# Second norm of a decoder block: the rounded and low parts of its transposed input made from SBUF, two tiles at a time

## The chip, the cores and the metric

One core of a Trainium2 chip runs the whole kernel. The core has TensorE (PE, matrix products into PSUM), VectorE (DVE), ScalarE (ACT), GpSimd (POOL) and SyncE (SP, which issues most transfers). Each engine works through its own list of instructions in order and waits on semaphores for the others. The metric is the device time of one execution in microseconds (us), the median of several runs. A profile of one execution gives every instruction's start and duration.

## What is computed

A decoder block on 512 positions of width 1024, in float32. What matters here is its second half: the attention and gMLP branches have been merged, and

```python
x = x + gate1 * (merged @ w_out)
h2 = rms_norm(x, norm2_g) * (1.0 + scale2) + shift2
f_g, f_u = jnp.split(h2 @ w_ffn_in, 2, axis=-1)      # w_ffn_in: 1024 x 5632
x = x + gate2 * ((jax.nn.silu(f_g) * f_u) @ w_ffn_out)
```

and a final RMSNorm. `scale2`, `shift2` and the gates come from the conditioning vector.

## The kernel before

**Products in three parts.** Every float32 product is made of three matmuls on fp32r numbers. An operand `a` is kept as a rounded part (`hi`, an fp32r copy of `a`) and a low part (`lo = a - hi`). `mm3` (L51 to L55) then adds `hi*hi`, one product of `hi` and `lo` (L54) and another (L55). So every tensor that TensorE reads has to be written twice, the rounded part mostly by ScalarE (an activation with function Copy), the low part mostly by VectorE (a subtraction).

**Weights.** The weights come in chunks of 128x1024 numbers through a stream with three raw buffers (L58 to L145). `ensure(i)` issues what has room and prepares all chunks up to `i`: ScalarE's rounded part at L110, the low part at L114, or, where a chunk's low part is marked "later", as a function kept in `do` that runs L112 when it is called. `W_F` are the four chunks of the first 256 columns of both halves of `w_ffn_in`; `WF0` lists them in order. All the other columns of `w_ffn_in` go through `s_issue(q)` (L1171) and `s_prep(q)` (L1194), for q = -2 to 17: each step takes two raw tiles, `ra` and `rb`, and makes sums and differences of their blocks (a Strassen-like scheme of seven block products), with ScalarE's rounded parts at L1206, L1215, L1223 and L1230 and VectorE's work at L1209 to L1211, L1218, L1219, L1226 and L1233. A raw buffer is free for the next transfer when its last reader is done.

**The output projection** (L1239 to L1272) runs over two halves of the positions (256 each) and, in each, over eight chunks of `w_out`, n_ = 0 to 7. In the second half the chunks come in the order of L1238: four for the first 512 columns, then four for the others. At the end of a column half `resid` (L1101) scales the product by the gate (L1104), adds it to the residual stream (L1105) and sums squares on ScalarE (L1106). `row_rstd` (L1108) makes the row's factor on VectorE (L1109) and GpSimd (L1110), and `norm2_x` (L1121) scales the rows into `xn`, one block of 128 rows on VectorE (L1128), the other on ScalarE (L1126). Between the chunks of the second half stand pieces of other work, written out by hand: the first half's norm and transposes, the preparation of `WF0`, and the start of `s_prep(-2)`.

**The transposes and what follows them** are `norm2_T` (L1130). For each of four banks k2 = 0 to 3 of PSUM (`x2T`, banks 4 to 7) TensorE makes four 128x128 transposes: two tiles kt = 2*k2 and 2*k2 + 1 of 128 columns, 256 positions each. From each tile three things are made:

- the rounded part `hi`, by ScalarE out of PSUM with scale and bias (L1159),
- `h2f`, the same in float32, by VectorE (L1164) or ScalarE (L1162), out of PSUM again,
- the low part `lo = h2f - hi`, by VectorE (L1165).

Instructions of two engines that read the same bank are ordered one behind the other by the kernel's tile framework. The banks of the first half are called in three pieces, at n_ = 2 of the second half's output projection, with the preparation of the chunk `WF0[2]` and `s_issue(-2)` between them. The second half's four banks are called as one, after the first chunk of the second weight half (L1477), and `pre[3]` (L1230, L1233) follows them.

**After it.** The first FFN columns are multiplied (`pf`, L1465 to L1491). `t_diff` (L1320) and `t_split` (L1328) then make the differences of `h2f` for the block products and split them into the tiles `tb`. Then comes the loop over q (L1500) with 20 steps of seven block products (`sprod`, 12 matmuls each), whose partial sums R are copied by ScalarE at L1533 to L1551 between the products that need them.

The order on every engine is that in which the instructions are written (a manual schedule), so moving a call moves its instructions on each engine's list.

Of the kernel before, what the change touches and what calls it, by code (L numbers as in the profile page):

```python
# [12 lines left out]
AF = mybir.ActivationFunctionType  # L13
OP = mybir.AluOpType
# [14 lines left out]
def block_kernel(ctx: ExitStack, tc: tile.TileContext, x, positions, w_ada, b_ada, w_in,  # L29
# [3 lines left out]
    T, V, A, P, SY = nc.tensor, nc.vector, nc.scalar, nc.gpsimd, nc.sync  # L33
# [8 lines left out]
    def bank(k, name="bank"):  # L42
        return psum.tile([128, 512], F32, name=name, tag=f"b{k}", bufs=1)

    def f(ap):
        return ap.bitcast(F32)
# [11 lines left out]
    stream, wseq, chunk = [], [], {}  # L58
# [58 lines left out]
    def ensure(upto):  # L117
        upto = min(upto, len(stream) - 1, st["limit"] - 1)
        while True:
            for i in range(st["prep"], min(st["prep"] + 16, len(stream), st["limit"])):  # L120
                if "raw" in stream[i]:
                    continue
                if room(i):
                    issue(i)
                elif stream[i]["kind"] == "w" or not stream[i]["mid"]:
                    break
            if st["prep"] > upto:
                break
            prep(st["prep"])
            st["prep"] += 1  # L130

    def room(i):
        e = stream[i]
        pend = stream[st["prep"]:i]
        if e["kind"] == "m" and e["early"]:
            return sum(p["kind"] == "m" for p in pend) < 8
        if e["kind"] == "m" and e["mid"]:
            return all(p["kind"] == "w" for p in pend) and len(pend) <= 1
        return sum(p["kind"] == "w" or not (p["early"] or p["mid"]) for p in pend) < RAWB


    def get(i, ahead=2):
        k = wseq.index(i)
        ensure(wseq[min(k + ahead, len(wseq) - 1)])
        return chunk[i]  # L145
# [128 lines left out]
    for i in range(4):  # L274
        t = base.tile([128, D], F32, name=f"x{i}", tag=f"X{i}", bufs=1)
# [202 lines left out]
    for kt in range(8):  # L478
        hi, lo = chunk[W1[kt]]
# [210 lines left out]
    def opt_a_mm(o, tk, hi, lo, kts, lhs, K, first=True):  # L690
        for j, kt in enumerate(kts):
            a = tuple(t[:, tk * 128:(tk + 1) * 128] for t in lhs[kt])
            mm3(o, a, (hi[:, j], lo[:, j]), kt == 0 and first, kt == K - 1, skip_group_check=True)
# [113 lines left out]
    for g in range(4):  # L807
        pb = [bank2(b, "pav") for b in nbanks()]
        for i in W_AV[g]:
# [10 lines left out]
            hi, lo = get(i)  # L820
# [280 lines left out]
    def resid(p, c0, n, slot, tk, gate):  # L1101
        cs_ = slice(c0, c0 + n)
        t = t512("rt")
        V.tensor_mul(t[:, :n], p, gate[:, cs_])  # L1104
        V.tensor_add(xt[tk][:, cs_], xt[tk][:, cs_], t[:, :n])  # L1105
        A.activation(t[:, :n], xt[tk][:, cs_], AF.Square, scale=1.0 / 32, accum_out=ss2[:, tk, slot:slot + 1])  # L1106
# [6 lines left out]
    HB = {}  # L1113
# [4 lines left out]
    h2f = {}  # L1118
# [8 lines left out]
            else:  # L1127
                V.tensor_scalar(xn[tk], xt[tk], r2[:, tk:tk + 1], None, op0=OP.mult)  # L1128

    def norm2_T(half, kts):  # L1130
        if kts[0]:
            pass
        elif half == 0:
            for kh in range(2):
                t = ffn[0].tile([128, 4, 256], F32, name="h2f", tag=f"F{kh}", bufs=1)
                for j in range(4):
                    h2f[kh * 4 + j, 0] = t[:, j]
                h2f["t", kh, 0] = [t[:, 0:2], t[:, 2:4]]
        else:
            for kh in range(2):  # L1140
                h2f["t", kh, 1] = []
                for q in range(2):
                    t = base.tile([128, 2, 256], F32, name="h2f", tag=f"S1_{kh * 2 + q}", bufs=1)
                    h2f["t", kh, 1].append(t)
                    for j in range(2):
                        h2f[kh * 4 + q * 2 + j, 1] = t[:, j]
        for k2 in kts:
            p = bank(4 + k2, "x2T")
            for k in range(2):
                kt = k2 * 2 + k  # L1150
                for e in range(2):
                    T.transpose(p[:, k * 256 + e * 128:k * 256 + (e + 1) * 128],
                                xn[2 * half + e][:, kt * 128:(kt + 1) * 128], ident)
            for k in range(2):
                kt = k2 * 2 + k
                g, s = Gc[:, 1, kt:kt + 1], Gc[:, 1, 8 + kt:9 + kt]
                src = p[:, k * 256:(k + 1) * 256]
                hi, lo = (t[:, kt % 4] for t in HB[kt // 4, half])
                A.activation(hi, src, AF.Identity, scale=g, bias=s)  # L1159
                hf = h2f[kt, half]  # L1160
                if kt % 4 == 3 or half and kt % 2:
                    A.activation(hf, src, AF.Identity, scale=g, bias=s)  # L1162
                else:
                    V.tensor_scalar(hf, src, g, s, op0=OP.mult, op1=OP.add)  # L1164
                V.tensor_sub(lo, hf, f(hi))  # L1165


    NQ = 18
# [2 lines left out]
    def s_issue(q):  # L1171
        if q >= NQ:
            return
        c0 = (2 + q // 2) * 256 + (DFF if q % 2 else 0)
        sraw[q] = []
        for kh in range(2):
            if q % 2 and kh:
                t = ffn[0].tile([128, 4, 2, 128], F32, name="raw", tag="F0" if q > 0 else "E5", bufs=1)
            else:
                t = base.tile([128, 4, 2, 128], F32, name="raw", tag="raw", bufs=RAWB)  # L1180
            SY.dma_start(t.rearrange("p j a n -> p j (a n)"),
                         w_ffn_in[kh * 512:(kh + 1) * 512, c0:c0 + 256].rearrange("(j p) n -> p j n", p=128))
            sraw[q].append(t)
# [53 lines left out]
    WF0 = W_F[0] + W_F[1]  # L1237
    OORD = (W_O, [W_O[n_] for n_ in (0, 2, 4, 5, 1, 3, 6, 7)])  # L1238
    for half in range(2):  # L1239
        po = {}  # L1240
        for n_, (h, i) in enumerate(OORD[half]):
            if half == 0:
                wch[i] = get(i, min(4, 7 - n_))
            hi, lo = wch[i]
            kts = stream[i]["kts"]
            if kts[0] == 0:
                po[h] = [bank(4 - 4 * half + 2 * h + e, "po") for e in range(2)]
            for e in range(2):
                opt_a_mm(po[h][e], 2 * half + e, hi, lo, kts, mT, 8)
            if kts[0] == 6:  # L1250
                for e in range(2):
                    resid(po[h][e], 512 * h, 512, h, 2 * half + e, gate_b[1])
            if half == 1:
                if n_ == 1:
                    for e in range(2):
                        row_rstd(e)
                    norm2_x(0)
                    ensure(WF0[1])
                if n_ == 2:
                    stream[WF0[2]]["lo"] = "later"  # L1260
                    norm2_T(0, (0, 1))
                    ensure(WF0[2])
                    norm2_T(0, (2,))
                    stream[WF0[2]]["do"]()
                    s_issue(-2)
                    norm2_T(0, (3,))
                if n_ == 3:
                    ensure(WF0[3])
                if n_ == 6:
                    pre = s_prep(-2)  # L1270
                    for fn in pre[0]:
                        fn()  # L1272
    pre[1][0]()
    for e in range(2, 4):
        row_rstd(e)
# [190 lines left out]
    for half in range(2):  # L1466
        o = slice(half * 256, (half + 1) * 256)
        for w in range(2):
            for ci, i in enumerate(W_F[w]):
                hi, lo = chunk[i]  # L1470
                for j, kt in enumerate(stream[i]["kts"]):
                    for m in range(2):
                        cc = slice(m * 128, (m + 1) * 128)
                        mm3(pf[w][m][:, o], (hi[:, j, cc], lo[:, j, cc]), tuple(t[:, j] for t in HB[ci, half]),
                            kt + half == 0, kt == 7, skip_group_check=True)
                if half == 0 and w == 1 and ci == 0:
                    norm2_T(1, range(4))  # L1477
                    for fn in pre[3]:
                        fn()
            if half == 0 and w == 1:  # L1480
                t_diff()
            if half == 1 and w == 0:
                s_issue(-1)
            if half == 1:
                if w == 0:
                    EV[w](0)(pf[w])
                t_split(w + 1)
                if w == 1:
                    t_split(3)
                    EV[w](0)(pf[w])  # L1490
                    t_split(4)  # L1491
# [8 lines left out]
    for q in range(-2, NQ):  # L1500
        g, u = 2 + q // 2, q % 2
# [178 lines left out]
    for h in range(2):  # L1680
# [4 lines left out]
        for n_, i in enumerate(ids[:-3] if h else ids):  # L1685
            kts = stream[i]["kts"]
            if h == 0:
                g_split(2 * n_ + 2)
            hi, lo = get(i)
# [4 lines left out]
            for tk in range(4):  # L1694
                if h and tk == 3:
                    for z in range(2):
                        c = slice(256 * z, 256 * z + 256)
# [12 lines left out]
        for tk in range(4):  # L1710
            for z in range(2) if tk == 3 else (None,):
                c = slice(0, 512) if z is None else slice(256 * z, 256 * z + 256)
# [68 lines left out]
```

## Time and profile before

| what | value |
|---|---|
| median of 3 runs | 843.1 us (842.83 to 843.16) |
| the profiled execution's own time | 843.06 us |
| its span, first to last instruction | 841.1 us |
| mean granted clock of TensorE | 0.998 |
| TensorE busy | 825.5 us, 98% |
| VectorE busy | 668.2 us, 79% |
| ScalarE busy | 403.5 us, 48% |
| GpSimd busy | 118.3 us, 14% |

A row of the timeline has the start in us from the span's start, the duration in us, the engine, the line of the kernel, the operation, the tile written and the tiles read, their shape, and how many instructions are merged (x16); in brackets stands how long the engine was idle before it, and what it waited for. A row of the groups has busy time and the mean duration of one in ns. A row of the waits says which engine and line waited for which, the total in us, how often, and the longest. A row of the chain has a start, the part of the time that the piece accounts for, and what it was. A row of the windows has the stretch, its length and, behind the comma, each engine's busy time (and its instructions). A busy TensorE doesn't mean one at its peak, since matmuls overlap each other; gaps between starts say more.

### The profile page before, as it was taken

The numbers are of one execution on the slowest core, as the hardware profiler recorded it, in microseconds if no ns is written. First come the engines' busy times: TensorE is split into PE (matmuls) and PEld (weight loads), VectorE is DVE, ScalarE is ACT, GpSimd is POOL, SyncE is SP. The second block draws the span as 40 slices with busy tenths as digits, with TensorE's granted clock in tenths as the row PEclk, the third lists the DMA queues.
The fourth block names the chain that finished last, engine by engine and source line by source line (L and its number), as shares of the span: only waits on it lengthen the run. The fifth ranks groups of instructions, "written<-read, shape, count | busy, mean of one in ns | idle before, by whom it ended". The sixth has DMA issues, their size and how long they took to land. (4 is left out here: it accounts for less than half of the span.)

```text
span 841.1 us, 12872 instructions
## 1 busy us (share of the span) xinstructions
PE 825.5 (98%) x4992; PEld 733.7 (87%) x4992; DVE 668.2 (79%) x1157; ACT 403.5 (48%) x706; POOL 118.3 (14%) x105
## 2 busy tenths in 40 slices
PE   7999999999999999999999999999999999999996
PEld 6888889988888888988888898999999999888885
DVE  7978799788899548886776679889998888985635
ACT  5664445322332227666334556555555555663322
POOL 2060022353354411002210000000000000000001
PEclk9999999999999999999999999999999999999999
DMA  9962362432346651037544122355553334143212
GB/s 297 311 190 71 96 199 78 127 92 84 109 144 198 197 154 51 26 108 243 175 151 150 58 69 76 108 157 164 164 159 105 101 101 151 51 139 104 82 50 101
DMA packets 95677, 109.09 MB, mean 130 GB/s; under 512 B 5617, under 2 KB 76273, under 8 KB 95617
## 3 DMA queue, kind: packets, MB, share of 16 engines
q1 hardware_dynamic: 92512, 101.37, 39.7%
q0 software_dynamic: 2384, 6.10, 2.0%
q8 instruction: 39, 0.64, 0.3%
q10 hardware_dynamic: 720, 0.82, 0.3%
q14 instruction: 22, 0.17, 0.1%
HBM read 105.90 MB, written 2.10 MB: 128 GB/s over the span
## 5 line engine op out<-in xcount | busy, mean ns | idle before, releaser
L110 ACT ACTIVATE hi<-raw 128x1024 fp32r<-128x1024 f32 (+2 forms) x83 | 85.6, 1035 | 105.5 <-PE pfo L55 34.9
L114 POOL TENSOR_TENSOR lo<-raw,hi 128x1024 fp32r<-128x1024 f32 x33 | 83.1, 2521 | 213.3 <-ACT hi L110 207.7
L114 DVE TENSOR_TENSOR lo<-raw,hi 128x1024 fp32r<-128x1024 f32 (+2 forms) x43 | 53.3, 1243 | 50.8 <-ACT hi L110 50.6
L53 PE MATMUL pb<-h,hi 128*128 128x512 f32 x192 | 76.4, 398 | 0.0
L54 PE MATMUL pb<-hl,hi 128*128 128x512 f32 x192 | 75.8, 395 | 0.0
L55 PE MATMUL pb<-h,lo 128*128 128x512 f32 x192 | 75.8, 395 | 0.0
L53 PE MATMUL R<-tb,hi 128*128 128x256 f32 x160 | 45.0, 281 | 1.5 <-ACT ps L1551 0.8
L55 PE MATMUL pfo<-hi,gs 128*128 128x512 f32 (+1 forms) x126 | 46.4, 369 | 0.0
L54 PE MATMUL pfo<-lo,gs 128*128 128x512 f32 (+1 forms) x126 | 46.4, 368 | 0.0
L53 PE MATMUL pfo<-hi,gs 128*128 128x512 f32 (+1 forms) x126 | 46.4, 368 | 0.0
L53 PE MATMUL R<-tb,sx 128*128 128x256 f32 x160 | 45.3, 283 | 0.5 <-ACT R L1533 0.5
L54 PE MATMUL R<-tb,sx 128*128 128x256 f32 x160 | 45.1, 282 | 0.0
L55 PE MATMUL R<-tb,sx 128*128 128x256 f32 x160 | 45.0, 281 | 0.0
L55 PE MATMUL R<-tb,lo 128*128 128x256 f32 x160 | 44.8, 280 | 0.0
L54 PE MATMUL R<-tb,hi 128*128 128x256 f32 x160 | 44.7, 280 | 0.0
L55 PEld LDWEIGHTS pb<-h,lo 128*128 128x128 f32 x192 | 36.0, 187 | 8.8
L54 PEld LDWEIGHTS pb<-hl,hi 128*128 128x128 f32 x192 | 36.0, 188 | 8.4
L53 PEld LDWEIGHTS pb<-h,hi 128*128 128x128 f32 x192 | 36.0, 188 | 8.3
L175 DVE SCALAR_TENSOR_TENSOR acc<-mraw,cols,acc 128x512 f32<-128x512 f32 x38 | 31.4, 827 | 9.6 <-DMA mraw<-in_w_ada_dram 8.8
L54 PE MATMUL pav<-lo,h 128*128 128x256 f32 x128 | 35.8, 279 | 0.0
L53 PE MATMUL pav<-hi,h 128*128 128x256 f32 x128 | 35.8, 279 | 0.0
L55 PE MATMUL pav<-hi,hl 128*128 128x256 f32 x128 | 35.7, 279 | 0.0
(377 smaller groups left out, 2652.3 us busy)
## 6 DMA issues: line engine op xcount, KB each, us to landing
raw<-in_w_ffn_in_dram SPq DMA_DIRECT2D x44, 512.0 KB, 4.2
raw<-in_w_in_dram SPq DMA_DIRECT2D x40, 512.0 KB, 3.9
mraw<-in_w_ada_dram SPq DMA_DIRECT2D x22, 512.0 KB, 4.1
raw<-in_w_ffn_out_dram SPq DMA_DIRECT2D x17, 512.0 KB, 3.9
s<-in_w_ada_dram SPq DMA_DIRECT2D x30, 256.0 KB, 5.5
raw<-in_w_ada_dram SPq DMA_DIRECT2D x10, 512.0 KB, 4.5
raw<-in_w_proj_a_dram SPq DMA_DIRECT2D x8, 512.0 KB, 4.7
raw<-in_w_proj_b_dram SPq DMA_DIRECT2D x8, 512.0 KB, 3.6
```

What stands on the lines that cost most here:

```text
L53: T.matmul(o, wh, rh, start=start, stop=False, **kw)
L54: T.matmul(o, wh, rlo, start=False, stop=False, **kw)
L55: T.matmul(o, wlo, rh, start=False, stop=stop, **kw)
L110: A.activation(hi[:, :m], e["raw"][:, :m], AF.Copy)
L114: e["lo"].tensor_sub(lo[:, :m], e["raw"][:, :m], f(hi[:, :m]))
L175: V.scalar_tensor_tensor(o, w, cs[:, j:j + 1], o, op0=OP.mult, op1=OP.add)
```

## The change

`norm2_T` takes a half and no list of banks. For each bank it makes `h2f` first, the first tile by VectorE, the second by ScalarE. Then ScalarE makes the rounded part of both tiles in one instruction of 512 columns, out of `h2f` in SBUF. VectorE's low part for both, also 512 columns, is put off until the next bank's `h2f` and rounded part are written, and the last one to the end. Work that stood between the calls is handed in as `also`, to be run behind a bank: `ensure(WF0[2])` behind the second, its low part and `s_issue(-2)` behind the third.

In the output projection of the second half the low part of `WF0[3]` is put off, and the start of `s_prep(-2)` (L1206, L1209 to L1211) moves from n_ = 6 to n_ = 3, ahead of that low part. That is one step ahead of the last residuals.

```diff
-    def norm2_T(half, kts):
-        if kts[0]:
-            pass
-        elif half == 0:
+    def norm2_T(half, also={}):
+        if half == 0:
...
-        for k2 in kts:
+        low = []
+        for k2 in range(4):
             p = bank(4 + k2, "x2T")
             for k in range(2):
                 kt = k2 * 2 + k
                 for e in range(2):
                     T.transpose(p[:, k * 256 + e * 128:k * 256 + (e + 1) * 128],
                                 xn[2 * half + e][:, kt * 128:(kt + 1) * 128], ident)
+            hf = h2f["t", k2 // 2, half][k2 % 2]
             for k in range(2):
                 kt = k2 * 2 + k
                 g, s = Gc[:, 1, kt:kt + 1], Gc[:, 1, 8 + kt:9 + kt]
                 src = p[:, k * 256:(k + 1) * 256]
-                hi, lo = (t[:, kt % 4] for t in HB[kt // 4, half])
-                A.activation(hi, src, AF.Identity, scale=g, bias=s)
-                hf = h2f[kt, half]
-                if kt % 4 == 3 or half and kt % 2:
-                    A.activation(hf, src, AF.Identity, scale=g, bias=s)
+                if k:
+                    A.activation(hf[:, k], src, AF.Identity, scale=g, bias=s)
                 else:
-                    V.tensor_scalar(hf, src, g, s, op0=OP.mult, op1=OP.add)
-                V.tensor_sub(lo, hf, f(hi))
+                    V.tensor_scalar(hf[:, k], src, g, s, op0=OP.mult, op1=OP.add)
+            hi, lo = (t[:, 2 * (k2 % 2):2 * (k2 % 2) + 2] for t in HB[k2 // 2, half])
+            A.activation(hi, hf, AF.Copy)
+            while low:
+                low.pop()()
+            low.append(lambda a=lo, b=hf, c=hi: V.tensor_sub(a, b, f(c)))
+            for fn in also.get(k2, ()):
+                fn()
+        low.pop()()
...
                 if n_ == 2:
                     stream[WF0[2]]["lo"] = "later"
-                    norm2_T(0, (0, 1))
-                    ensure(WF0[2])
-                    norm2_T(0, (2,))
-                    stream[WF0[2]]["do"]()
-                    s_issue(-2)
-                    norm2_T(0, (3,))
+                    norm2_T(0, {1: [lambda: ensure(WF0[2])],
+                                2: [lambda: stream[WF0[2]]["do"](), lambda: s_issue(-2)]})
                 if n_ == 3:
+                    stream[WF0[3]]["lo"] = "later"
                     ensure(WF0[3])
-                if n_ == 6:
                     pre = s_prep(-2)
                     for fn in pre[0]:
                         fn()
+                    stream[WF0[3]]["do"]()
...
-                    norm2_T(1, range(4))
+                    norm2_T(1)
```

More of the change, by code (lines that the diff above doesn't have):

```diff
@@ L1128, in norm2_x @@
                 V.tensor_scalar(xn[tk], xt[tk], r2[:, tk:tk + 1], None, op0=OP.mult)
-    def norm2_T(half, kts):
-        if kts[0]:
-            pass
-        elif half == 0:
+    def norm2_T(half, also={}):
+        if half == 0:
             for kh in range(2):
                 t = ffn[0].tile([128, 4, 256], F32, name="h2f", tag=f"F{kh}", bufs=1)
-                for j in range(4):
-                    h2f[kh * 4 + j, 0] = t[:, j]
                 h2f["t", kh, 0] = [t[:, 0:2], t[:, 2:4]]
@@ L1144, in norm2_T @@
                     h2f["t", kh, 1].append(t)
-                    for j in range(2):
-                        h2f[kh * 4 + q * 2 + j, 1] = t[:, j]
-        for k2 in kts:
+        low = []
+        for k2 in range(4):
             p = bank(4 + k2, "x2T")
```

## The prediction

> **What bounds the kernel now.** I read the waits of the whole run first, to see where TensorE stands still, then its timeline around those places, then the chain of waits back from them, and last the timelines of VectorE and ScalarE. All that TensorE ever waited for:
>
> ```profile
> PE warm L440 <- DMA cst<-in_consts_dram: 4.8, 1, 4.8
> PE R L53 <- ACT R L1533: 1.2, 2, 0.7
> PE modS L413 <- DVE accw L175: 1.0, 2, 0.5
> PE R L53 <- ACT ps L1551: 0.8, 1, 0.8
> PE x2T L1152 <- ACT xn L1126: 0.6, 1, 0.6
> ```
>
> The first and third belong to the start of the run (the constants' load, the first modulation). The other four waits (columns: total, times, longest) and three that stand only in the weight-load row below lie within 35 us of each other, around the transposes of the second norm:
>
> ```profile
> PEld pf L54 <- DVE h L1165: 0.7, 3, 0.3
> ```
>
> ```profile
> 471.96 1.91 PE L1152 MATMUL x2T<-cst,xn 128*128 128x128 f32 x16
> ...
> 487.45 0.39 PE L55 MATMUL po<-wx,ml 128*128 128x512 f32 x1
> 487.68 0.28 PE L53 MATMUL pf<-h,wx 128*128 128x256 f32 x1
> ...
> 496.25 0.27 PE L1152 MATMUL x2T<-cst,xn 128*128 128x128 f32 x1
> 497.17 1.86 PE L1152 MATMUL x2T<-cst,xn 128*128 128x128 f32 x15 [0.64 <-ACT xn L1126]
> ...
> 528.75 0.28 PE L55 MATMUL R<-tb,sx 128*128 128x256 f32 x1
> 529.50 0.38 PE L53 MATMUL R<-tb,sx 128*128 128x256 f32 x1 [0.48 <-ACT R L1533]
> 529.73 0.28 PE L54 MATMUL R<-tb,sx 128*128 128x256 f32 x1
> ```
>
> What they cost TensorE is counted from starts, since a matmul's shown length overlaps the next. From 487.68 to 496.25 the code has 72 matmuls of 256 columns: 0.119 us each. Fifteen transposes in 1.86 with a last one of 0.27 make 0.114 each. Between 487.68 and 529.50 the code has 300 such matmuls (96 of the first half, 96 of the second, 84 of step q = -2, 24 of q = -1) and 16 transposes: 300 x 0.119 + 16 x 0.114 = 37.5 us. The two starts lie 41.8 apart. Lost: 4.3 us, and the last restart (0.23 to the next start instead of 0.12) makes **4.4 us**. Of it 0.8 is the wait for xn (0.92 between starts, less 0.11), 0.7 the last wait (0.75 + 0.23 less 0.24), and 2.9 the waits between.
>
> Who makes TensorE wait is seen in the chain of waits, which runs off TensorE from 483 until 529.5:
>
> ```profile
> 499.32 0.47 DVE h2f L1164
> 499.81 0.56 ACT h L1159
> 500.38 0.46 ACT h2f L1162
> 500.83 0.47 ACT h L1159
> 501.32 0.55 DVE h2f L1164
> ...
> 507.09 0.96 ACT hi L1230
> 508.07 1.23 DVE lo L1233
> ```
>
> The two engines take turns on each bank of x2T: ScalarE's rounded part, VectorE's h2f, ScalarE again. Four banks take 507.09 - 499.32 = 7.8 us, though neither engine is busy for all of it. Behind L1233 VectorE has no room to catch up: 18.01 of 18.29 us busy.
>
> ```profile
> 508.07:526.36 18.29, 18.01 (x26) 1.00 0.15 51
> ```
>
> So the late L1233 is handed on to tb, to ScalarE's copies of R and ps, and to TensorE.
>
> **The change part by part.** TensorE's order is unchanged; matmuls are neither added nor removed, nor moved. The instruction rows of norm2_T, and the nearest rows for the new pair-wide ones (an fp32r copy of 128x512 from SBUF, L303, and a 128x512 low part, L304):
>
> ```profile
> L303 ACT ACTIVATE tb<-h2f 128x512 fp32r<-128x512 f32 x8 | 4.5, 622 | 2.0 <-DVE h2f L1323 1.6 <-DVE h2f L1325 0.4
> L1159 ACT ACTIVATE h<-x2T,Gc 128x256 fp32r<-128x256 f32 x8 | 4.5, 561 | 3.1 <-DVE h2f L1164 3.1
> ```
>
> ```profile
> L1165 DVE TENSOR_TENSOR h<-h2f,h 128x256 fp32r<-128x256 f32 x8 | 3.4, 425 | 2.6 <-ACT h2f L1162 2.5
> L1164 DVE TENSOR_SCALAR h2f<-x2T,Gc 128x256 f32<-128x256 f32 x4 | 2.2, 542 | 0.1
> ```
>
> ```profile
> 514.22 2.72 ACT L303 ACTIVATE tb<-h2f 128x512 fp32r<-128x512 f32 x5 [0.36 <-DVE h2f L1325]
> ```
>
> ```profile
> 514.77 3.70 DVE L304 TENSOR_TENSOR tb<-h2f,tb 128x512 fp32r<-128x512 f32 x6
> ```
>
> Back to back, five copies in 2.72 are 0.53 apart, six low parts in 3.70 about 0.60 apart with 0.68 for the last; 256 columns on either engine are about 0.47 apart (chain pieces). In the second half ScalarE's 8 + 4 activations (12 x 0.47 = 5.6) become 4 h2f and 4 pair-wide copies (4 x 0.47 + 4 x 0.53 = 4.0). VectorE's 4 + 8 (4 x 0.47 + 8 x 0.35, the 0.425 rows less the same overlap = 4.7) become 4 + 4 (4 x 0.47 + 4 x 0.60 = 4.3). More than the work, the waits shrink: a bank is handed over once (VectorE to ScalarE) instead of twice.
>
> *Half 0, start and end.*
>
> ```profile
> 472.60 0.56 ACT L1159 ACTIVATE h<-x2T,Gc 128x256 fp32r<-128x256 f32 x1 [2.08 <-PE x2T L1152]
> ```
>
> ```profile
> 483.18 0.43 DVE L1165 TENSOR_TENSOR h<-h2f,h 128x256 fp32r<-128x256 f32 x1 [0.63 <-ACT h2f L1162]
> 483.52 0.68 DVE L1104 TENSOR_TENSOR rt<-po,gate1b 128x512 f32<-128x512 f32 x1
> ...
> 491.12 0.68 DVE L1104 TENSOR_TENSOR rt<-po,gate1b 128x512 f32<-128x512 f32 x1
> ```
>
> ```profile
> 495.97 1.15 ACT L1126 ACTIVATE xn<-xr,sm 128x1024 f32<-128x1024 f32 x1 [0.34 <-POOL sm L1110]
> ```
>
> Bank 0 is ready 0.64 after the first transpose (471.96 to 472.60). I walk the new order with these rows and 0.04 per hand-over. VectorE: h2f at 472.6 and 473.1; low part 0 at 474.4 (behind ScalarE's h2f 473.2 and copy 473.8); h2f 2 at 475.0; low part 1 at 475.5; the weight's low part L112 at 476.5, when ScalarE's 1024-column copy (0.96 to the next, as L1230) is done; h2f 3 at 477.7; low parts at 478.1 and 479.5. So L1104 starts at 480.1, not 483.52: 3.4 earlier. Its po ended long before.
>
> Next come the moved pieces. Between the residuals of the first column half and those of the second, VectorE holds the same four instructions as before: L112 (late now) and L1209 to L1211, which step from n_ = 6 to 3 but on VectorE only change places with L112. L1209 now heads the queue, and L1210 waits for ScalarE's sa, behind two squares and the weight copy; that costs VectorE about as much standing as its wait for ScalarE's wx cost ahead of L114 before. What is queued behind is the second L1104, then both reductions, xn and the transposes. I take its gain as 3.4 to 3.5: 487.6 instead of 491.12. The po matmul that L1104 needs ended its e = 0 part six matmuls before 487.45 + 0.39, about 486.5, so TensorE doesn't hold it. xn for the last rows then goes from 495.97 to 492.5 and ends at 493.6; TensorE reaches the transposes at 496.25. The 0.8 us wait goes, with 2.6 us in hand. L1209 also needs its data: the second s_issue transfer leaves when L112 frees its buffer, at 477.7, and lands 3.6 (4.8 at most) later, by 482.5; VectorE gets there at 482.7.
>
> ```profile
> DMA to landing us min/median/max: 3.6/3.6/4.8
> ```
>
> SP's queue keeps its order, GpSimd's too. The lost cover of L112 is nil: TensorE first reads that low part behind the second transposes, at 496.25 + 16 x 0.114 = 498.
>
> *Half 1.* Transposes start at 496.25; bank 0 is ready at 496.9. Starts, us:
>
> ```
> pair  h2f VectorE  h2f ScalarE  copy ScalarE  low part VectorE (end)
> 0        496.9        497.5        498.1        498.7 (499.4)
> 1        497.4        498.6        499.2        499.9 (500.5)
> 2        499.3        499.9        500.5        501.2 (501.9)
> 3        500.5        501.0        501.6        502.3 (503.0)
> ```
>
> L1230 starts at 502.2 instead of 507.09 and L1233 at 503.3 instead of 508.07: **4.8 us earlier**, half of it from the earlier start (496.9 for 499.3), half from the shorter turns (5.3 us for 7.8). TensorE needs low part 0 at 501, the last at 505.3: those three waits go with about 2 us in hand.
>
> From L1233 on VectorE's order is as before, and so everything it feeds comes 4.8 earlier, while TensorE comes at most 4.4 earlier. ScalarE's table load for Silu no longer waits for TensorE, which helps the same way. The tightest place is the last wait: ScalarE's R would be ready at 529.5 - 4.8 = 524.7; TensorE would ask for it at 528.75 + 0.12 - 3.7 = 525.2. In hand: **0.4 us**, and as much at every later step, since before 529.5 is the last wait in the list.
>
> Sum: nothing is added to TensorE; 0.8 + 2.9 + 0.7 = 4.4 us of its waits go. The profiled execution took 843.06 us (span 841.1, 2.0 around it), the median is 843.1, so they may be used for one another. Forecast: 843.06 - 4.4 = **838.7 us**.
>
> One operation has no row: ScalarE waiting for its own h2f before it copies the pair. Below: nothing (back to back). Above: 0.2 each, half the overlap of two ScalarE activations counted again, five such hops on the way to L1230, so 1.0 late. I take 0.04, the hand-over between engines. Less than nothing is excluded, as the copy needs the written tile. At the upper end 0.6 of it passes the 0.4 in hand: 839.3.
>
> [...]
>
> **The rivals.**
> 1. *Part of the waits come back.* VectorE's L1233 is later than walked (own-tile waits, or ScalarE's h2f held up by a copy ahead of it). For: only 0.4 us in hand and no idle time on VectorE behind it. Against: every hop has a row. From 0.4 late on, each us costs one; 0.4 to 2.5 later gives 839.0 to 841.2; its middle, 840.
> 2. *The change doesn't do what it says.* Both engines still read each bank. If the turns stay in series, a pair takes 0.54 + 0.56 + 0.62 + 0.68 and four hand-overs, 2.6 us, and four 10.2 against 7.8; the earlier start is eaten, L1230 is where it was, and only the wait for xn goes: 842.3. Against: the written order puts each low part behind the next bank's h2f.
> 3. *Slower: VectorE stands at L1209.* It now waits for the transfers before L112 and the residuals. Price: the landing's delay, one for one. xn has 2.6 us in hand over a sa that is ready at 485.1, so TensorE waits again if the data land after 487; all of the gain is gone at 491.5, and it is 0.2% slower from 493.2, 15.5 us after the issue at 477.7. The rows show 4.8 at most.
>
> **How the numbers follow.** Forecast (838.2 to 839.0): 0.72. Rival 1: 0.18. Rival 2: 0.06. Rival 3: 0.04. What a measurement can tell from no change is about 0.2%, 1.7 us. The forecast and rival 1 lie faster than that: 0.90; rival 2 is the same: 0.06; rival 3 slower: 0.04. The range 838.0 to 840.6 takes in the bounds of the own-tile wait and most of rival 1.
>
> **What would show it.** Right: no wait of TensorE for xn, h, R or ps in the list; L1104 at about 480.1 and 487.6; the transposes as one group of 16 at 496.25; L1230 near 502.2, L1233 near 503.3; TensorE never off the chain after 484. Wrong: a wait for R or ps near 521 to 526 (rival 1), four banks taking as long as before (rival 2), or VectorE idle ahead of L1209 for a DMA (rival 3). The forecast falls if TensorE waits anywhere after 530, where it waited for nothing before.

## The result, and the profile after

| | us, median | runs |
|---|---|---|
| before | 843.06 | 6 (842.83 to 843.38) |
| changed | 838.08 | 6 (837.91 to 838.31) |

The changed kernel takes 0.9941 of the time before, with a 95% interval from 0.9928 to 0.9954: faster by 5.0 us, where 4.4 was forecast (838.7, range 838.0 to 840.6). The median lies inside the range by 0.1 us, and 0.1 us under the bracket of the forecast itself (838.2 to 839.0). The profiled execution took 838.10 us, with a span of 836.2.

All waits of TensorE in the changed kernel, over the whole run (engine and line waited for: total, times, longest):

```profile
PE warm L440 <- DMA cst<-in_consts_dram: 4.6, 1, 4.6
PE modS L413 <- DVE accw L175: 0.2, 1, 0.2
```

The waits for R, ps and xn are gone, and so is the one for h among the weight loads. In the windows view TensorE is busy without a gap from 461 to 530, where it was busy for 66.27 of 69.00 us before (first row before, second row changed):

```profile
461.00:530.00 69.00, 66.27 (x445) 59.94 (x444) 53.13 (x85) 39.29 (x73) 3.65 (x5) 1.00 0.23 73
```

```profile
461.00:530.00 69.00, 69.00 (x485) 64.21 (x484) 54.73 (x78) 41.01 (x71) 3.65 (x5) 1.00 0.24 78
```

VectorE's timeline, at the places the prediction named: end of the first half and the first residual; the step that moved; second residual; the second half up to L1233.

```profile
479.28 0.69 DVE L1162 TENSOR_TENSOR h<-h2f,h 128x512 fp32r<-128x512 f32 x1 [0.70 <-ACT h L1159]
479.89 0.68 DVE L1104 TENSOR_TENSOR rt<-po,gate1b 128x512 f32<-128x512 f32 x1
...
482.54 0.69 DVE L1209 TENSOR_TENSOR raw<-raw 128x512 f32<-128x512 f32 x1
484.89 0.69 DVE L1210 TENSOR_TENSOR sa<-raw,sa 128x512 fp32r<-128x512 f32 x1 [1.66 <-ACT sa L1206]
...
487.36 0.68 DVE L1104 TENSOR_TENSOR rt<-po,gate1b 128x512 f32<-128x512 f32 x1
...
496.68 1.00 DVE L1157 TENSOR_SCALAR h2f<-x2T,Gc 128x256 f32<-128x256 f32 x2 [1.11 <-PE x2T L1147]
498.52 0.69 DVE L1162 TENSOR_TENSOR h<-h2f,h 128x512 fp32r<-128x512 f32 x1 [0.84 <-ACT h L1159]
...
502.09 0.69 DVE L1162 TENSOR_TENSOR h<-h2f,h 128x512 fp32r<-128x512 f32 x1 [0.43 <-ACT h L1159]
503.04 1.23 DVE L1233 TENSOR_TENSOR lo<-raw,hi 128x1024 fp32r<-128x1024 f32 x1 [0.26 <-ACT hi L1230]
```

This run reached the first transposes 0.21 us earlier than the run before (below), so 0.2 is to be added when comparing with the prediction's times. L1104 then stands at 480.1 (forecast 480.1) and 487.6 (487.6), L1230 at 502.2 (502.2), L1233 at 503.25 (503.3). L1209 waits for no DMA. ScalarE's xn and L1230, and the sixteen transposes:

```profile
492.21 1.15 ACT L1126 ACTIVATE xn<-xr,sm 128x1024 f32<-128x1024 f32 x1 [0.34 <-POOL sm L1110]
...
501.96 1.05 ACT L1230 ACTIVATE hi<-raw 128x1024 fp32r<-128x1024 f32 x1
```

```profile
496.04 1.91 PE L1147 MATMUL x2T<-cst,xn 128*128 128x128 f32 x16
```

xn is finished at 493.4 and needed at 496.0; the transposes run as one group.

To separate this stage from the rest of the run I measure each trace from the start of the first x2T transposes to the start of the last matmul. Before and after, the last matmul, and the first transposes of the changed kernel (those of before stand in the prediction):

```profile
833.87 0.28 PE L55 MATMUL pfo<-hi,gs 128*128 128x256 f32 x1
```

```profile
829.02 0.28 PE L55 MATMUL pfo<-hi,gs 128*128 128x256 f32 x1
```

```profile
471.75 1.91 PE L1147 MATMUL x2T<-cst,xn 128*128 128x128 f32 x16
```

833.87 - 471.96 = 361.91 before, 829.02 - 471.75 = 357.27 after: **4.64 us** shorter. The rest of the 5.0 lies ahead of the changed code (0.21 in these two traces) and in the spread of runs.

The same distance is taken from every trace below, and beside it a second one: from the first x2T transposes to the first instruction of `t_diff`, with which VectorE starts as soon as it is through L1233. These are its rows, before and changed:

```profile
509.22 0.68 DVE L1323 TENSOR_TENSOR h2f<-h2f 128x512 f32<-128x512 f32 x1
```

```profile
504.19 0.68 DVE L1320 TENSOR_TENSOR h2f<-h2f 128x512 f32<-128x512 f32 x1
```

```
kernel                         first   last    distance  shorter  t_diff  distance  earlier
                               x2T     matmul            by                         by
before                         471.96  833.87  361.91     -       509.22  37.26      -
changed                        471.75  829.02  357.27    4.64     504.19  32.44     4.82
changed, again                 471.50  828.78  357.28    4.63     503.94  32.44     4.82
second half only               471.63  831.09  359.46    2.45     506.42  34.79     2.47
first half and step ahead only 471.85  832.06  360.21    1.70     507.39  35.54     1.72
no step ahead                  472.09  829.36  357.27    4.64     504.52  32.43     4.83
no step ahead, again           471.79  829.06  357.27    4.64     504.22  32.43     4.83
step ahead alone               471.41  833.29  361.88    0.03     508.64  37.23     0.03
low part not put off           471.65  834.71  363.06   -1.15     510.04  38.39    -1.13
rounded parts from the bank    472.36  830.25  357.89    4.02     505.58  33.22     4.04
one more L1233                 471.69  830.03  358.34    3.57     505.38  33.69     3.57
two more L1233                 471.64  831.26  359.62    2.29     506.59  34.95     2.31
```

Wherever VectorE is earlier by up to 4.04 us, or later, the kernel is shorter or longer by just as much, to 0.02 us. In the four traces where VectorE is 4.82 or 4.83 earlier, the saving stops at 4.63 or 4.64, and no wait of TensorE is left in this stretch.

### The profile page after: what moved, and what is told of

It reads as the page before. It is cut to its first block, busy times and chain, and to the rows that moved or that the text cites. A ratio compares the mean times of both kernels' runs of the same rounds, so it can differ in the third digit from the quotient of the medians.

```text
span 836.2 us, 12860 instructions
## 1 busy us (share of the span) xinstructions
PE 824.3 (99%) x4992; PEld 733.8 (88%) x4992; DVE 666.7 (80%) x1147; ACT 401.8 (48%) x700; POOL 118.3 (14%) x105
## 4 chain that ended last, share of the span: by engine, by line
PE 95%; DMA 2%; SPq 1%; issue 0%; ACT 0%; DVE 0%; POOLq 0%; POOL 0%; ACTq 0%
PE pb L53 9%; PE pb L55 9%; PE pb L54 9%; PE R L53 8%; PE R L54 8%; PE R L55 8%; PE pfo L55 4%; PE pfo L53 4%; PE pfo L54 4%; PE pav L54 2%; PE pav L53 2%; PE pav L55 2%; PE pgb L53 2%; PE po L54 2%; PE pgb L54 2%; PE pgb L55 2%
## 5 line engine op out<-in xcount | busy, mean ns | idle before, releaser
L114 POOL TENSOR_TENSOR lo<-raw,hi 128x1024 fp32r<-128x1024 f32 x33 | 83.3, 2528 | 212.7 <-ACT hi L110 199.1
L114 DVE TENSOR_TENSOR lo<-raw,hi 128x1024 fp32r<-128x1024 f32 (+2 forms) x43 | 53.3, 1244 | 51.0 <-ACT hi L110 50.9
```

Source lines behind the costliest of these rows:

```text
L114: e["lo"].tensor_sub(lo[:, :m], e["raw"][:, :m], f(hi[:, :m]))
```

## The experiments

The theory: the time follows VectorE's arrival at L1233, because behind it VectorE has almost no idle time (18.01 of 18.29 us busy before) and TensorE depends on what it hands on, until TensorE has no waits left to lose. The last two columns of the table bear on it in every run. The rivals: each wait falls by itself; fewer or wider instructions are the gain; reading the bank once is the gain; the step ahead is what brings xn in time.

**The second half alone.** The kernel before, with the changed `norm2_T` added as `new_T` and called for half 1 only:

```diff
-                    norm2_T(1, range(4))
+                    new_T(1)
```

> Only the second half's transposed input is made in the new way; the first half's, and the place of the first s_prep step, stay as before. Theory (the gain is how much earlier VectorE gets through L1233, as far as TensorE had waits to lose): VectorE comes to the second half's banks as late as before (499.3) and leaves them 5.3 us on instead of 7.8, so L1233 is 2.4 us earlier than 508.1; the wait for xn stays, the waits for low parts go, of the last three waits a part stays: 843.1 - 2.4 = 840.7 us. Rival (each of the seven waits falls or stays by itself, and all but the one for xn belong to the second half): 843.1 - 3.7 = 839.4 us.

Measured: 840.25 us beside 842.93 before, ratio 0.9967 (0.9954 to 0.9979); 2.45 us in the trace, against 2.4 by the theory. TensorE's waits in this kernel, without the one at the start of the run:

```profile
PE x2T L1185 <- ACT xn L1126: 0.7, 1, 0.7
PE R L53 <- ACT R L1571: 0.5, 1, 0.5
PE R L53 <- ACT ps L1589: 0.2, 1, 0.2
```

The wait for xn is there. Of the three late waits the first is gone, the one for ps stands in part (0.2 of 0.8) and the last one in full: what VectorE gained is used up by the earlier waits. The rival, which would let every wait but xn's fall, is out by 0.9 us in the median and 1.2 in the trace.

**The first half and the step ahead alone.** The reverse: the changed kernel, with the old `norm2_T` added as `old_T`:

```diff
-                    norm2_T(1)
+                    old_T(1, range(4))
```

> The reverse: the first half in the new way and the moved s_prep step, the second half's banks as before. Theory: the transposes come at once, VectorE starts the second half's banks at 497.3 instead of 499.2 but takes turns as long as before, so L1233 is 1.8 us earlier: 843.1 - 1.8 = 841.3 us, with no wait for xn and none for low parts, but with waits for R and ps. Theory and first run together: the two gains add up to 4.2, and the whole change stops at what TensorE had to lose. Rival (each wait by itself): only the wait for xn, 0.8, goes: 842.3 us.

Measured: 841.17 us beside 842.93, ratio 0.9979 (0.9970 to 0.9988); 1.70 us in the trace. Of TensorE's waits, those in the stretch in question:

```profile
PE R L53 <- ACT R L1568: 1.2, 2, 0.7
PE R L53 <- ACT ps L1586: 0.8, 1, 0.8
```

These late waits are as long as before the change, though the early ones for xn and h are gone. By itself this would also fit a rival in which the waits for h fall with the first half; the rival as priced (842.3) is out by 1.1 us. The table speaks for one chain: VectorE is through L1233 1.72 us earlier, and the kernel is 1.70 shorter. The two halves add up to 4.15, not to 4.64. The old order begins a bank with ScalarE's rounded part, and VectorE's first h2f starts behind it:

```profile
497.38 0.54 DVE L1202 TENSOR_SCALAR h2f<-x2T,Gc 128x256 f32<-128x256 f32 x1 [1.71 <-ACT h L1197]
```

In the changed order it starts 0.64 after the first transpose (496.68), here 1.2 after it (496.15). So what the second half gains in the whole change includes some of an earlier start that the old order can't use.

**Without the step ahead, and the step ahead alone.** Two kernels. In the first the changed kernel gets the old place back:

```diff
                 if n_ == 3:
-                    stream[WF0[3]]["lo"] = "later"
                     ensure(WF0[3])
+                if n_ == 6:
                     pre = s_prep(-2)
                     for fn in pre[0]:
                         fn()
-                    stream[WF0[3]]["do"]()
```

> The changed kernel with the start of s_prep(-2) back at n_ = 6 and the low part of WF0[3] not put off. Theory: VectorE waits for ScalarE's wx ahead of L114 instead of for sa ahead of L1210, about as long, and comes to the second L1104 0.1 us later (487.45 for 487.36); xn has 2.6 us in hand: 838.1 us, no change against the changed kernel. Rival (the step ahead is what brings xn in time): the wait for xn is back, 838.9 us or more.

In the second the kernel before gets the new place and nothing else.

> The kernel before with nothing but the step ahead: s_prep(-2) starts at n_ = 3, ahead of the low part of WF0[3], which is put off. Theory: VectorE stands ahead of L1210 instead of ahead of L114, the second L1104 moves from 491.1 to 491.0: 843.0 us, no change. Rival (it is what brings xn in time): 842.3 us.

Measured: 838.50 us (ratio 0.9947, 0.9933 to 0.9960), and 842.93 (0.9999, 0.9990 to 1.0008). The distances are 4.64 and 0.03. The first median lay 0.4 above the first one of the changed kernel, on another chip, so both were run again side by side:

> The changed kernel itself, beside the next run on one chip, as its control. In the traces the stretch from the first transposes to the last matmul is 4.64 us shorter than before; all else in the difference of the medians (5.0 in the first measurement) lies ahead of it, in waits at the start of the run that the change does not touch. Theory: 4.3 to 5.0 us under the kernel before, by chip and run.

> The changed kernel without the step ahead, on the same chip as its control. Theory: within 0.2 us of the control, since its stretch from the first transposes to the last matmul had the same length to 0.01 us. Rival (the step ahead is worth the 0.5 us by which the two first measurements differ): 0.4 to 0.6 us over the control.

Measured: 838.13 us for the changed kernel (0.9941, 0.9927 to 0.9954) and 838.28 without the step (0.9941, 0.9928 to 0.9953). The step ahead is worth nothing that could be measured. VectorE stands for ScalarE about as long either way: 1.66 us ahead of L1210 with the step (the row above), 1.74 ahead of L114 without it:

```profile
484.71 1.23 DVE L114 TENSOR_TENSOR wx<-raw,wx 128x1024 fp32r<-128x1024 f32 x1 [1.74 <-ACT wx L110]
```

**The low part not put off.** Same instructions as the changed kernel, other order:

```diff
-            while low:
-                low.pop()()
-            low.append(lambda a=lo, b=hf, c=hi: V.tensor_sub(a, b, f(c)))
+            V.tensor_sub(lo, hf, f(hi))
```

> The changed kernel, but each bank's low part is issued straight behind its rounded part, not one bank later. Theory (the order decides, not the instructions, which are the same): VectorE's next h2f stands behind a low part that waits for ScalarE, and a bank takes h2f, h2f, copy and low part in series, about 2.45 us; four take 9.8 instead of 7.8 before and 5.3 in the changed kernel. The first half then ends as late as before (483.6), the second half starts as late as before, and L1230 comes about 1.3 us later than 507.1: 844.4 us, slower than before. Rival (fewer and wider instructions are the gain): 838.1 to 838.5 us.

Measured: 843.84 us beside 843.06, ratio 1.0010 (1.0001 to 1.0019); in the trace 1.15 us longer than before and 5.8 longer than the changed kernel. VectorE's second half (three of its rows):

```profile
501.23 0.54 DVE L1156 TENSOR_SCALAR h2f<-x2T,Gc 128x256 f32<-128x256 f32 x1
503.06 0.69 DVE L1159 TENSOR_TENSOR h<-h2f,h 128x512 fp32r<-128x512 f32 x1 [1.30 <-ACT h L1158]
503.67 0.54 DVE L1156 TENSOR_SCALAR h2f<-x2T,Gc 128x256 f32<-128x256 f32 x1
```

From one h2f to the next are 2.44 us (2.45 expected), of which VectorE stands 1.30 with the low part at the head of its queue, while the next bank is ready (the last transposes had ended at 498.6) and the h2f behind it can't start. In this order the fewer and wider instructions are no gain; the kernel loses 0.1%, an interval that just clears 1.

**The rounded parts from the bank.** The changed order, but the rounded part of each tile out of PSUM, as before:

```diff
...
-            A.activation(hi, hf, AF.Copy)
+                A.activation(hi[:, k], src, AF.Identity, scale=g, bias=s)
...
```

> The changed kernel, but the rounded parts are made as before, one tile at a time out of the bank with scale and bias (so the bank is read twice for each tile), behind VectorE's h2f; low parts pair-wide and put off as in the change. Theory (one hand-over for each bank and the low part put off are the gain; the source is not): ScalarE has three activations of 0.47 for each bank instead of 0.47 and 0.53, L1230 comes 0.8 us later than in the changed kernel, of which 0.3 is in hand: 838.6 us. Rival (reading the bank once is the gain): most of it is lost, 840.5 us or more.

Measured: 838.69 us beside 843.06, ratio 0.9949 (0.9936 to 0.9961); 4.02 us of the 4.64 remain. Part of a wait is back:

```profile
PE R L53 <- ACT R L1530: 0.4, 1, 0.4
```

Making the rounded parts from SBUF, one instruction for two tiles, is worth 0.6 us. The other 4.0 stay with what this run leaves as changed: VectorE first, one hand-over for each bank, and the low part two tiles wide and one bank late. The run before shows that nothing of it is left when the low part is not put off; VectorE first and the wider low part were not tried alone.

**More work on VectorE.** The changed kernel with `pre[3][1]()` (L1233) called once more, then twice more, behind the loop that calls it:

```diff
                     for fn in pre[3]:
                         fn()
+                    pre[3][1]()
```

> The changed kernel with L1233 of the first s_prep step run twice: VectorE has one more instruction of 1.2 us (1.15 to the next) in front of t_diff, nothing else. Theory (0.3 to 0.4 us in hand at the last wait, VectorE without idle time behind it): 1.15 - 0.3 = 0.85 us slower than the changed kernel, 838.9 us, with TensorE's wait for R back. Rival (TensorE is the bound with room to spare): 838.1 us. Rival (VectorE is already the bound): 839.3 us.

> As the run before, with L1233 run three times: two more instructions, 2.3 us. Theory: 2.3 - 0.3 = 2.0 us slower than the changed kernel, 840.1 us. Rival (room to spare): under 0.5 us. The difference of the two runs is what a late us costs once the room is gone: 1.15 by the theory.

Measured: 839.28 us (0.9955, 0.9941 to 0.9968) and 840.54 (0.9970, 0.9959 to 0.9982). By distance 1.07 and 2.35 us longer than the changed kernel. The two instructions took 2.48 together, the three 3.74:

```profile
502.97 2.48 DVE L1233 TENSOR_TENSOR lo<-raw,hi 128x1024 fp32r<-128x1024 f32 x2 [0.26 <-ACT hi L1230]
```

```profile
502.93 3.74 DVE L1233 TENSOR_TENSOR lo<-raw,hi 128x1024 fp32r<-128x1024 f32 x3 [0.26 <-ACT hi L1230]
```

So one more is 1.25 or 1.26 us (I had taken 1.15), and it costs 1.07 the first time, 1.28 the second. With one more, the last wait for R is back:

```profile
PE R L53 <- ACT R L1531: 0.5, 1, 0.5
```

The room at the last wait is about 0.2 us, and behind it 1.26 us more on VectorE made the kernel 1.28 longer. The first median, 839.28, lies on the rival that gave no room at all (839.3, with 1.15 for the instruction). That VectorE is not yet the bound in the changed kernel rests on the traces: TensorE has no wait there, and 1.25 us more on VectorE cost 1.07.

## Why the prediction was right

- **What bounds it.** Right: late VectorE and ScalarE, met by TensorE at seven places. The table shows one chain, not seven separate waits: the kernel follows VectorE's arrival at `t_diff` in every run, down to the two in which nothing but VectorE's work there was added.
- **What TensorE had to lose.** 4.4 forecast, 4.64 measured. This is the term that was mis-sized. For the 300 matmuls and 16 transposes between 487.68 and 529.50 I had put 37.5 us without waits. In the changed kernel nothing is lost there, and the same stretch takes 37.28:

```profile
487.47 0.28 PE L53 MATMUL pf<-h,wx 128*128 128x256 f32 x1
...
497.71 0.36 PE L53 MATMUL pf<-h,wx 128*128 128x256 f32 x1
...
524.75 0.28 PE L53 MATMUL R<-tb,sx 128*128 128x256 f32 x1
```

  The transposes, up to the start of the next matmul, take 1.67 (from 496.04), not 16 x 0.114 = 1.82, a price read from a group that started behind a wait. The 300 matmuls take 35.61, 0.1187 each for 0.119. With 37.28 in the prediction's own sum, 41.82 - 37.28 and 0.1 for the last restart are 4.64. The forecast of the time was short by 0.6: 0.2 from here, 0.2 from ahead of the changed code, the rest the spread of runs. The last two were not forecast, and without them the time would stand near 838.4.
- **Half 0.** Right to 0.1 us: 480.1 and 487.6 on the common scale. The step ahead costs and gains nothing, shown by itself and by its absence. The prediction had it in one sum with the first half, and had read from VectorE's two waits that they would be about equal.
- **Half 1.** Right: L1233 was 4.8 us earlier, half by the earlier start and half by shorter turns. The low parts, at 498.7, 499.9, 501.2 and 502.3 with the 0.2 added, start where the prediction's table has them. In the separate runs VectorE was 1.72 and 2.47 earlier, 0.63 less than 4.82 in sum; 0.59 of it is the old order's later first h2f (1.23 behind the first transpose, not 0.64).
- **The hand-over of ScalarE to itself.** The unknown had the bounds 0 and 0.2, the upper one an estimate that the rows do not give: a copy and the activation behind it overlap by 0.09 (0.63 less 0.54, below). In the changed kernel's timeline the h2f of the second half's first bank and the copy behind it:

```profile
497.26 0.57 ACT L1155 ACTIVATE h2f<-x2T,Gc 128x256 f32<-128x256 f32 x1 [2.95 <-DVE h2f L1157]
497.86 0.63 ACT L1159 ACTIVATE h<-h2f 128x512 fp32r<-128x512 f32 x1
498.40 0.55 ACT L1155 ACTIVATE h2f<-x2T,Gc 128x256 f32<-128x256 f32 x1
```

  497.26 + 0.57 to 497.86 is 0.03: near the lower end, and close to the 0.04 that was taken. The copy's successor, which doesn't read what the copy writes, follows 0.54 later, so the copy's 0.63 is not paid in full.
- **The room of 0.4 us** was too large, by the same term: it was 4.8 less 4.4, and measured it is 4.82 less 4.64, 0.2, as the runs with more work confirm (1.25 less 1.07). ScalarE's R was ready at 524.43 (the row below), and its matmul started at 524.75; the distance is 0.3 at best.

```profile
524.07 0.36 ACT L1530 ACTIVATE R<-R 128x256 f32<-128x256 f32 x1
```

  It didn't matter here. In the run with one more L1233 it did: 838.9 expected, 839.28 measured, about 0.1 of it from the room, 0.1 from the instruction's price, the rest the spread of runs.
- **The rivals.** The first (waits come back) is real and close: it takes 0.2 us more on VectorE. The second (turns in series) did not come about, and its price was judged too kindly: I had it at 842.3, faster than before, and the kernel that does this took 843.84, slower than before, since the first half is as late as before (its L1104 starts 11.55 us behind the first transpose, 11.56 before) and the wait for xn stays (0.5 us). The third (L1209 for its data) was not tried; VectorE went into L1209 without waiting.

## What to carry to other kernels

Where two engines take turns on a tile, look at what stands at the head of each queue. With the new instructions, a dependent one put off by one turn was worth 5.8 us here (363.06 against 357.27), and the rounded parts' fewer and wider instructions 0.6; what putting off would do with the old instructions was not tried. The saving was the smaller of two numbers, how much earlier the late engine gets through and how much the bound engine was waiting, so measure both before you cost an edit. Count lost time from starts of matmuls, since the waits listed (0.6 + 0.7 + 1.2 + 0.8 = 3.3 us) left out 1.3 of the 4.64 us that came back. And price work without waits from a stretch that no wait touches: the mis-sized term came from a group behind one.

## What was not expected of the hardware

The waits cost TensorE more than their idle time in the list: 3.3 us of listed waits became 4.64 us of time. The row at 529.50 before shows both parts. It starts 0.75 behind the last start, 0.63 more than an undisturbed step of 0.12, where the list has 0.48; and the step to the next start is 0.23, not 0.12. Six of the seven waits have such a slow first step (0.22 or 0.23).

A second L1233 directly behind the first, on the same tile, starts 1.25 us later, where the next instruction behind a single L1233 starts after 1.15 (504.19 - 503.04 in the changed kernel). What makes the difference was not tried.
